# RWKV-7 bulk products of the chunks on 64x64 quarters of TensorE, in two closed bursts per head pair

## The chip, the cores and the metric

The kernel runs on one core of a Trainium2 chip. The metric is the device time of one execution in microseconds (us); for the kernel before it is the median of three runs. Five engines work side by side: TensorE (PE in the profile; its weight loads are shown apart, as PEld), VectorE (DVE), ScalarE (ACT), GpSimd (POOL) and SyncE (SP), which issues transfers. Each works through its own list of instructions in order; semaphores hold an instruction until what it reads is there. Differences under about 0.2% of the time can't be told from no change here.

## The reference

One decoder block on 512 tokens of width 2048, in float32. A projection `z = rms_norm(x) @ w_in` feeds two mixers, RWKV-7 time mixing and windowed attention, which are gated, merged, projected and followed by a gated ConvFFN. The change lies in the RWKV-7 part, with 16 heads of 64 channels:

```python
def step(state, inp):                       # state: (heads, 64, 64)
    r_t, k_t, v_t, w_t, ka_t, kb_t = inp    # ka = -kk, kb = kk * a
    sa = einsum('bhvk,bhk->bhv', state, ka_t)
    state = state * w_t[:, :, None, :] + sa[..., None] * kb_t[:, :, None, :] \
            + v_t[..., None] * k_t[:, :, None, :]
    y = einsum('bhvk,bhk->bhv', state, r_t)
    return state, y
_, y = lax.scan(step, state0, xs)           # over 512 tokens
y = group_norm(y) * gn_w + gn_b
out = (y + bonus) * g
```

## The kernel before

**Tiling.** The scan over 512 tokens is done in 8 chunks of 64 tokens (`NCH` = 8, `C` = 64), and two heads are worked on together, one in partitions 0 to 63 and one in 64 to 127: 8 head pairs. `early(p)` projects r, k and v of pair `p` and prepares decays; `late(p)` does the chunks; `final(p)` does the group norm and the output. The loop is `late(p)`, `early(p+1)`, `final(p)` and then three gate projections, and this repeats for all pairs.

**What `late` does.** For each chunk, L700 multiplies the decayed k and b vectors (`BKK`) with the decayed a and r vectors (`BAR`); L704 masks the result into four tiles: `BX` and `MD` (a head's own part) and `OA` and `MO` (which stand in the other head's rows). All of them are 128x128 per chunk; the half that doesn't belong to a head is zero. A triangular inverse is then found in `BX` by five doubling levels in float16 (L761 and L762 with weights `AI`, then with `BT`, then the transposes of L790). L737 writes the centred values `VV` with the two heads swapped, so that they meet `OA`, `MO` and `KO`.

**Bulk products.** Three sums have no dependence from chunk to chunk: `GV` = `OA` x `VV` and `KV` = `KO` x `VV` (both L724, 8 matmuls each), and the output `y` (L821 `MO` x `VV`, L822 `MD` x `UU`, L824 `BAR` x `SS`; 8 + 8 + 7 matmuls into one PSUM tile). Each is a 128x128 weight, half of it zeros, against 64 columns. `KO` shares its buffer with `OA`, so L748 and L749 clear it on POOL after the product with `OA` is done.

**The chain.** Chunk after chunk: `psG` (L802), add on DVE (L804), `psU` (L808), copy `UU` on ACT (L809), `psS` (L815), add on DVE (L816) to the next state `SS`. The products for `y` of a chunk stand in the program behind the chain's loop.

**What sets the order.** The instructions of an engine are put in order when the kernel is built, by a scheduler that simulates costs; instructions that are handed to `pin` keep their order of writing among themselves. The scheduler fills the places where the small products would wait with matmuls of the projections (`acc`, L260 to L262, 128x512), of which there are always some left: 288 per pair from the next pair's r, k, v and three gates. Weights of the projections come by DMA as `raw` and are split by ACT (`whi`, L243) and DVE (`wlo`, L244).

Of the kernel before, what the change touches and what calls it, by code (L numbers as in the profile page):

```python
# [8 lines left out]
F32 = mybir.dt.float32  # L9
# [3 lines left out]
AF = mybir.ActivationFunctionType  # L13
ALU = mybir.AluOpType
# [4 lines left out]
P = 128  # L19
# [3 lines left out]
C = 64  # L23
NCH = S // C
# [110 lines left out]
def block_kernel(ctx: ExitStack, tc: tile.TileContext, d: Dims, a: dict, out: bass.AP):  # L135
    nc = tc.nc
    act, dve, pool, pe, sync = nc.scalar, nc.vector, nc.gpsimd, nc.tensor, nc.sync
# [34 lines left out]
    K = {nm: cst[:, o - P : o - P + n] for nm, (o, n) in CONST_AT.items() if o}  # L172
# [27 lines left out]
    pin = tc.keep_in_program_order  # L200
# [80 lines left out]
    if True:  # L281
# [7 lines left out]
        with tc.tile_pool(name="x0_ps", bufs=5, space=PSUM) as ps0:  # L289
# [36 lines left out]
            r = scales(0)  # L326
# [3 lines left out]
            for k in range(NK):  # L330
                columns(0, k)
                if k == NK // 2 - 1:
                    r = scales(1)
# [55 lines left out]
        with ExitStack() as pt:  # L389
# [31 lines left out]
            for t in range(NKV):  # L421
# [16 lines left out]
                ps = small().rearrange("p (n c) -> p n c", c=P)  # L438
# [24 lines left out]
            for g in range(NHK):  # L463
# [7 lines left out]
                for n in range(NT):  # L471
# [15 lines left out]
                    st = ap_.tile([P, 4, GQ], F32, name="st", tag="st", bufs=2)  # L487
# [14 lines left out]
                    for kb in kbs:  # L502
                        ps = small().rearrange("p (h c) -> p h c", c=P)
# [6 lines left out]
                    ps = small()[:, : GQ * HD].rearrange("p (h c) -> p h c", c=HD)  # L510
                    for h in range(GQ):
                        for kb in kbs:
                            pe.matmul(ps[:, h], pT[:, kb, h], vt[:, n - 1 + kb, g * HD : (g + 1) * HD],
                                      start=kb == kbs[0], stop=kb == kbs[-1])
                    ot = ap_.tile([P, GQ, HD], F32, name="ot", tag="ot", bufs=2)
                    dve.tensor_tensor(ot, ps, rc.unsqueeze(2).to_broadcast([P, GQ, HD]), op=ALU.mult)
                    ps = small()[:, : GQ * HD].rearrange("p (j c) -> p j c", c=P)
# [7 lines left out]
        with ExitStack() as pr:  # L525
# [21 lines left out]
            def bulk():  # L547
                return blk.tile([P, S], F32, name="bulk", tag="bulk")
# [15 lines left out]
            for i in range(NG):  # L564
                acc = ztile(d.c_gd + i * P)
                t = wtile("lw")
# [12 lines left out]
            BAR = bd.tile([P, NCH, 2, 2, C], F32, name="BAR")  # L579
            pool.memset(BAR[0:C, :, :, 1], 0.0)  # L580
            pool.memset(BAR[C:P, :, :, 0], 0.0)
            MO, MD = (bd.tile([P, NCH, P], F32, name=n) for n in ("MO", "MD"))
            KD = bdtile("KD")
            SS, UU, VV, KV = (bd.tile([P, NCH, C], F32, name=n) for n in ("SS", "UU", "VV", "KV"))
            Et = bd.tile([P, NCH, C + 1], F32, name="Et")
# [9 lines left out]
            def r3(ap, c=C):  # L595
                return ap.rearrange("p (n c) -> p n c", c=c)
# [10 lines left out]
            def lora(ps, w, lo, hi):  # L607
                for i in range(lo, hi):
                    pe.matmul(ps, w[:, i], ads[:, i], start=i == lo, stop=i == hi - 1)

            def early(p):
                wl = lp.tile([P, 2 + NG, P], F32, name="wl", tag="wl", bufs=2)
# [55 lines left out]
            def late(p, st):  # L668
# [21 lines left out]
                def mb(nm, n, h=None):  # L690
                    m = K[nm] if h is None else K[nm][h[0] : h[1]]
                    return m.unsqueeze(1).to_broadcast([m.shape[0], n, m.shape[-1]])

                BKE = wk.tile([P, NCH, P], F32, name="BKE", tag="BKE")
                dve.tensor_tensor(BKE, BKK, ee.unsqueeze(2).to_broadcast([P, NCH, P]), op=ALU.mult)
                OA = wk.tile([P, NCH, P], F32, name="OA", tag="ko")
                for n0 in range(0, NCH, 2):
                    ps = bulk()
                    for j in range(2):
                        pe.matmul(ps[:, j * 4 * C : (j + 1) * 4 * C], BKK[:, n0 + j],  # L700
                                  BAR[:, n0 + j].rearrange("p a h c -> p (a h c)"), start=True, stop=True)
                    pq = ps.rearrange("p (n a c) -> p n a c", n=2, a=2)
                    for t, a, nm in ((BX, 0, "own"), (OA, 0, "other"), (MD, 1, "own"), (MO, 1, "other")):
                        dve.tensor_tensor(t[:, n0 : n0 + 2], pq[:, :, a], mb(nm, 2)[:, :, a * P : (a + 1) * P], op=ALU.mult)  # L704
                for g in range(2):
                    ns = slice(g * HN, (g + 1) * HN)
                    for h, (lo, hi) in enumerate(HV):
# [10 lines left out]
                    dve.tensor_scalar(BX[C:P, ns, C:P], tt[C:P, ns], 1.0 / SG, None, op0=ALU.mult)  # L718
                    for i in range(2):
                        dve.tensor_tensor(BT[:, i, ns], AI[:, i, ns], mb("t1bd", HN), op=ALU.mult)  # L720
                def bulk_mm(dst, l, r):
                    ps = bulk()
                    for n in range(NCH):
                        pe.matmul(r3(ps)[:, n], l(n), r(n), start=True, stop=True)  # L724
                    act.activation(dst, r3(ps), AF.Copy)

                ps = bulk()
                for t in range(NT):
                    ts = slice(t * P, (t + 1) * P)
# [2 lines left out]
                dve.reduce_sum(vm, r3(ps), axis=AX.X)  # L732
                dve.tensor_scalar(vm, vm, -1.0 / HD, None, op0=ALU.mult)
                for a, (fl, fh) in enumerate(HV):
                    for h in range(2):
                        ol, oh = HV[1 - h]
                        dve.tensor_tensor(VV[ol:oh, a::2], r3(ps)[fl:fh, h::2],  # L737
                                          vm[fl:fh, h::2].unsqueeze(2).to_broadcast([C, NT, C]), op=ALU.add)
                GV = wk.tile([P, NCH, C], F32, name="GV", tag="yt")
                bulk_mm(GV, lambda n: OA[:, n], lambda n: VV[:, n])  # L740
                for g in range(2):
                    ns = slice(g * HN, (g + 1) * HN)
                    ps = bulk().rearrange("p (n c) -> p n c", c=P)
                    for j in range(HN):
                        pe.transpose(ps[:, j], BKE[:, g * HN + j], ident)
                    if g == 0:
                        KO = wk.tile([P, NCH, P], F32, name="KO", tag="ko")
                        pool.memset(KO[0:C, :, 0:C], 0.0)  # L748
                        pool.memset(KO[C:P, :, C:P], 0.0)  # L749
                    for h, (lo, hi) in enumerate(HV):  # L750
                        ol, oh = HV[1 - h]
                        act.activation(KD[lo:hi, ns, lo:hi], ps[lo:hi, :, lo:hi], AF.Copy)
                        act.activation(KO[lo:hi, ns, ol:oh], ps[lo:hi, :, ol:oh], AF.Copy)

                bulk_mm(KV, lambda n: KO[:, n], lambda n: VV[:, n])

                def mm3(wt, both, high):
                    ps = bulk()
# [40 lines left out]
                for n in range(NCH):  # L799
                    if n:  # L800
                        ps = chn.tile([P, C], F32, name="psG", tag="chn")
                        pe.matmul(ps, BAR[:, n, 0].rearrange("p h c -> p (h c)"), SS[:, n], start=True, stop=True)  # L802
                        G = wk.tile([P, C], F32, name="G", tag="G", bufs=2)
                        dve.tensor_tensor(G, GV[:, n], ps, op=ALU.add)  # L804
                    else:
                        G = GV[:, 0]
                    ps = chn.tile([P, C], F32, name="psU", tag="chn")
                    pe.matmul(ps, BX[:, n], G, start=True, stop=True)  # L808
                    act.activation(UU[:, n], ps, AF.Copy)  # L809
                    if n == NCH - 1:  # L810
                        break
                    if n:
                        dve.scalar_tensor_tensor(KV[:, n], SS[:, n], ee[:, n : n + 1], KV[:, n], op0=ALU.mult, op1=ALU.add)
                    ps = chn.tile([P, C], F32, name="psS", tag="chn")
                    pe.matmul(ps, KD[:, n], UU[:, n], start=True, stop=True)  # L815
                    dve.tensor_tensor(SS[:, n + 1], KV[:, n], ps, op=ALU.add)  # L816

                ps = bulk()
                for n in range(NCH):
                    dst = r3(ps)[:, n]  # L820
                    pe.matmul(dst, MO[:, n], VV[:, n], start=True, stop=False)  # L821
                    pe.matmul(dst, MD[:, n], UU[:, n], start=False, stop=n == 0)  # L822
                    if n:
                        pe.matmul(dst, BAR[:, n, 1].rearrange("p h c -> p (h c)"), SS[:, n], start=False, stop=True)  # L824
                yt = wk.tile([P, NCH, C], F32, name="yt", tag="yt")
                act.activation(yt, r3(ps), AF.Copy)
                return ag, bon, yt

            def final(p, st):
                ag, bon, yt = st  # L830
                sq = wk.tile([P, NCH, C], F32, name="gn", tag="gn")
                act.activation(sq, yt, AF.Square)
                ss = wk.tile([P, NCH], F32, name="ssy", tag="ssy")
                dve.reduce_sum(ss, sq, axis=AX.X)
                rs = rsqrt_small(wk, ss, 1.0 / HD, GN_EPS)
                yd = wk.tile([P, NT, 2, C], F32, name="yd", tag="ko")
                for a, (al, ah) in enumerate(HV):
                    for h, (lo, hi) in enumerate(HV):
                        dve.tensor_tensor(yd[al:ah, :, h], yt[lo:hi, a::2],
                                          rs[lo:hi, a::2].unsqueeze(2).to_broadcast([C, NT, C]), op=ALU.mult)  # L840
                ps = bulk()
                for t in range(NT):
                    pe.transpose(ps[:, t * P : (t + 1) * P], yd[:, t].rearrange("p h c -> p (h c)"), ident)
                yc = wtile("gn")
                dve.scalar_tensor_tensor(yc, ps, col("gn_w", p), bon, op0=ALU.mult, op1=ALU.add)
                ps = bulk()
                lora(ps, ag, 1, 1 + NG)
                dve.tensor_tensor(yc, yc, ps, op=ALU.mult)
                pool.dma_start(o_rw_d[p], yc)

            st = early(0)
# [599 lines left out]
```

## Time and profile before

| | us |
|---|---|
| median of 3 runs (2877.06 to 2877.37) | 2877.19 |
| the profiled execution: its time | 2876.5 |
| the profiled execution: its span | 2874.7 |
| PE busy in the span | 2810.6 |
| DVE busy | 1957.0 |
| ACT busy | 1323.9 |
| one head pair (the third, from one L700 to the next) | 102.5 |

The span is from the first to the last instruction. A pair's length is read from the starts of its first matmul of L700, which come every 102.5 us from the second pair on. The page's "busy" counts overlapping matmuls once; their ends are modelled, so a matmul's price is better read from the distance between starts. A float32 matmul stands in the trace as two records (two passes, each with a weight load of its own), a float32r or float16 one as one. The granted TensorE clock is full in all of the span but its first part.

### The profile page before, as it was taken

Reading aid. Unit: us, or ns where it says so; the run is one execution under the profiler, and the core shown is the slowest. Engines: PE = TensorE matmul, PEld = TensorE weight load, DVE = VectorE, ACT = ScalarE, POOL = GpSimd, SP = SyncE. Lnnn points to the kernel's source line nnn. Section 1 sums busy time; section 2 is a strip of 40 time slices with the busy share of each in tenths; the row PEclk is TensorE's granted clock in tenths of the full one; section 3 lists DMA queues with packets and bytes.
Section 4 is the critical chain, followed back from the end, with each engine's and each line's share of the span. In section 5 each row is a group of like instructions: output and inputs, shape, how many; then the busy total and the mean of one; then the engine's idle time right before and its main releaser. Section 6 shows DMA issues by size and latency. Waiting matters only on the chain.

```text
span 2874.7 us, 46847 instructions
## 1 busy us (share of the span) xinstructions
PE 2810.6 (98%) x17970; PEld 2455.0 (85%) x17970; DVE 1957.0 (68%) x3388; ACT 1323.9 (46%) x2191; POOL 235.1 (8%) x319
## 2 busy tenths in 40 slices
PE   7999999999999999999999899999999999999999
PEld 6888777777777777788888899999999999888887
DVE  5566666767776675345668787777778777655655
ACT  5345344435434434322456445455555545544444
POOL 0101000000000001111000010101011010000000
PEclk9999999999999999999999999999999999999999
DMA  6855666666656657878777788888888887877775
GB/s 199 228 158 148 182 163 168 160 161 153 166 144 162 174 152 183 269 237 272 258 262 209 211 237 229 222 233 244 230 226 226 242 236 217 315 246 241 258 254 190
DMA packets 223857, 608.35 MB, mean 212 GB/s; under 512 B 24577, under 2 KB 44689, under 8 KB 222609
## 3 DMA queue, kind: packets, MB, share of 16 engines
q1 hardware_dynamic: 156096, 432.86, 46.6%
q0 software_dynamic: 36832, 134.24, 24.2%
q10 hardware_dynamic: 30704, 38.27, 3.8%
q8 instruction: 141, 2.31, 0.3%
q14 instruction: 84, 0.68, 0.1%
HBM read 554.59 MB, written 174.40 MB: 254 GB/s over the span
## 4 chain that ended last, share of the span: by engine, by line
PE 59%; DMA 3%; DVE 2%; ACT 1%; issue 1%; ACTq 0%; SPq 0%; DVEq 0%
PE X L1152 17%; PE X L1019 10%; PE Y L1019 9%; PE Y L1152 8%; PE Z L1152 4%; PE acc L262 3%; PE acc L260 3%; PE acc L261 3%; DMA raw<-in_w_z_dram 1%; DMA raw<-in_w_dn_dram 1%; DMA raw<-in_w_b_dram 0%; DMA raw<-in_w_up_dram 0%; DVE wlo L1135 0%; PE ps_t L1083 0%; DMA gate_d<-gt 0%
## 5 line engine op out<-in xcount | busy, mean ns | idle before, releaser
L260 PE MATMUL acc<-xhi,whi 128*128 128x512 f32 x1120 | 454.0, 405 | 1.9 <-ACT whi L243 1.9
L262 PE MATMUL acc<-xhi,wlo 128*128 128x512 f32 x1120 | 449.4, 401 | 3.2 <-DVE wlo L244 3.2
L261 PE MATMUL acc<-xlo,whi 128*128 128x512 f32 x1120 | 452.1, 404 | 0.0
L243 ACT ACTIVATE whi<-raw 128x512 fp32r<-128x512 f32 x352 | 219.8, 629 | 468.1 <-PE acc L261 355.0
L244 DVE TENSOR_TENSOR wlo<-raw,whi 128x512 fp32r<-128x512 f32 x352 | 240.3, 689 | 233.0 <-ACT whi L243 214.8
L1012 DVE TENSOR_TENSOR wlo<-raw,whi 128x1024 fp32r<-128x1024 f32 x210 | 257.1, 1224 | 205.3 <-ACT whi L1011 205.3
L1011 ACT ACTIVATE whi<-raw 128x1024 fp32r<-128x1024 f32 x210 | 222.6, 1060 | 289.7 <-PE X L1019 147.8
L1152 PE MATMUL X<-b,whi 128*128 128x256 f32 x1472 | 270.4, 284 | 2.3 <-DVE u L1172 0.9
L1152 PE MATMUL X<-t,whi 128*128 128x256 f32 x1408 | 259.9, 285 | 9.9 <-DVE u L1172 9.4
L1135 DVE TENSOR_TENSOR wlo<-raw,whi 128x1024 fp32r<-128x1024 f32 x176 | 215.0, 1223 | 77.8 <-ACT whi L1134 77.7
L1152 PE MATMUL Y<-t,whi 128*128 128x256 f32 x1408 | 257.1, 283 | 0.0
L262 PEld LDWEIGHTS acc<-xhi,wlo 128*128 128x128 f32 x1120 | 211.2, 189 | 45.7 <-DVE wlo L244 8.2
L260 PEld LDWEIGHTS acc<-xhi,whi 128*128 128x128 f32 x1120 | 211.7, 189 | 38.3 <-ACT whi L243 3.2
L261 PEld LDWEIGHTS acc<-xlo,whi 128*128 128x128 f32 x1120 | 211.6, 189 | 38.1 <-issue 2.2
L1134 ACT ACTIVATE whi<-a 128x1024 fp32r<-128x1024 f32 x132 | 139.4, 1056 | 218.7 <-DVE a L1128 214.6
L1152 PEld LDWEIGHTS X<-b,whi 128*128 128x128 f32 x1472 | 230.7, 193 | 3.1 <-issue 2.4
L1152 PEld LDWEIGHTS X<-t,whi 128*128 128x128 f32 x1408 | 221.7, 194 | 10.4 <-DVE u L1172 6.8
L1152 PEld LDWEIGHTS Y<-t,whi 128*128 128x128 f32 x1408 | 219.6, 192 | 0.0
L1152 PE MATMUL X<-b,wlo 128*128 128x256 f32 x736 | 209.1, 284 | 2.1 <-DVE wlo L1135 2.1
L1135 DVE TENSOR_TENSOR wlo<-a,whi 128x1024 fp32r<-128x1024 f32 x132 | 161.7, 1225 | 69.8 <-ACT whi L1134 69.2
L1152 PE MATMUL X<-t,wlo 128*128 128x256 f32 x704 | 200.4, 285 | 0.0
L1152 PE MATMUL Y<-t,wlo 128*128 128x256 f32 x704 | 199.2, 283 | 0.0
(777 smaller groups left out, 5987.4 us busy)
## 6 DMA issues: line engine op xcount, KB each, us to landing
raw<-in_w_up_dram SPq DMA_DIRECT2D x180, 512.0 KB
raw<-in_w_z_dram SPq DMA_DIRECT2D x288, 256.0 KB
s_dn<-in_w_dn_dram POOLq DMA_DIRECT2D x88, 512.0 KB, 6.8
raw<-in_w_up_dram POOLq DMA_DIRECT2D x88, 512.0 KB, 8.7
raw<-s_dn SPq DMA_DIRECT2D x88, 512.0 KB
raw<-in_w_dn_dram SPq DMA_DIRECT2D x66, 512.0 KB
a<-in_w_up_dram SPq DMA_DIRECT2D x48, 512.0 KB
s_dn<-in_w_dn_dram SPq DMA_DIRECT2D x44, 512.0 KB
```

The lines of the kernel that those rows point to most:

```text
L243: pin(act.activation(hi, raw, AF.Copy))
L244: pin(dve.tensor_tensor(lo, raw, hi.bitcast(F32), op=ALU.subtract))
L260: pe.matmul(acc, whi[:, j], xhi[:, k], start=first, stop=False)
L261: pe.matmul(acc, whi[:, j], xlo[:, k], start=False, stop=False)
L262: pe.matmul(acc, wlo[:, j], xhi[:, k], start=False, stop=last)
L1011: act.activation(whi, wr, AF.Copy)
L1012: dve.tensor_tensor(wlo, wr, whi.bitcast(F32), op=ALU.subtract)
L1019: pe.matmul(dst, l[:, q, ts], r[:, es], start=fst and j == 0, stop=lst and j == 2, skip_group_check=True)
L1134: pin(act.activation(hi, t, AF.Copy))
L1135: pin(dve.tensor_tensor(lo, t, hi.bitcast(F32), op=ALU.subtract))
L1152: pin(pe.matmul(ps, l[:, k], r[:, k], start=start and k + i == 0, stop=last and i == 2, skip_group_check=True))
```

## The change

The bulk products use 64x64 quarters of the array. A new helper `heads_mm` issues two matmuls for each one before, first for the head in partitions 64 to 127, then for that in 0 to 63; each multiplies 64 rows by 64 columns and writes 64 partitions. `OA` and `MO` become one compact tile `AM`, into which the masking (now L715 and L719) moves each part to the partitions of its own head; `KO` becomes compact too, in a buffer that needs no clearing, and `VV` is written with the heads at home. All of these matmuls are pinned, and with them the chain's `psU`. `KV` and `GV` are issued one behind the other as one burst in front of the doubling levels; the whole of `y` is taken out of the chain's neighbourhood, into `final`, as a second burst behind the chain, in reversed order of chunks, so that the last `UU` is waited for first. The chain's own products stay on the whole array.

```diff
-            MO, MD = (bd.tile([P, NCH, P], F32, name=n) for n in ("MO", "MD"))
+            MD = bd.tile([P, NCH, P], F32, name="MD")
+            AM = bd.tile([P, NCH, 2, C], F32, name="AM")
...
+            def heads_mm(dst, l, r, start, stop):
+                for h, (lo, hi) in reversed(list(enumerate(HV))):
+                    w = l[lo:hi] if l.shape[-1] == C else l[lo:hi, lo:hi]
+                    pin(pe.matmul(dst[lo:hi], w, r[lo:hi], start=start, stop=stop, skip_group_check=True))
+
+            def bulk_mm(dst, l, r):
+                ps = bulk()
+                for n in reversed(range(NCH)):
+                    heads_mm(r3(ps)[:, n], l(n), r(n), True, True)
+                act.activation(dst, r3(ps), AF.Copy)
...
-                    for t, a, nm in ((BX, 0, "own"), (OA, 0, "other"), (MD, 1, "own"), (MO, 1, "other")):
-                        dve.tensor_tensor(t[:, n0 : n0 + 2], pq[:, :, a], mb(nm, 2)[:, :, a * P : (a + 1) * P], op=ALU.mult)
+                    for t, a in ((BX, 0), (MD, 1)):
+                        dve.tensor_tensor(t[:, n0 : n0 + 2], pq[:, :, a], mb("own", 2)[:, :, a * P : (a + 1) * P], op=ALU.mult)
+                    for h, (lo, hi) in enumerate(HV):
+                        rs = slice(*HV[1 - h])
+                        mk = K["other"].rearrange("p (a c) -> p a c", a=2)[rs, :, lo:hi]
+                        dve.tensor_tensor(AM[lo:hi, n0 : n0 + 2], pq[rs, :, :, lo:hi],
+                                          mk.unsqueeze(1).to_broadcast([C, 2, 2, C]), op=ALU.mult)
...
-                    for h in range(2):
-                        ol, oh = HV[1 - h]
-                        dve.tensor_tensor(VV[ol:oh, a::2], r3(ps)[fl:fh, h::2],
+                    for h, (lo, hi) in enumerate(HV):
+                        dve.tensor_tensor(VV[lo:hi, a::2], r3(ps)[fl:fh, h::2],
...
-                GV = wk.tile([P, NCH, C], F32, name="GV", tag="yt")
-                bulk_mm(GV, lambda n: OA[:, n], lambda n: VV[:, n])
...
-                        KO = wk.tile([P, NCH, P], F32, name="KO", tag="ko")
-                        pool.memset(KO[0:C, :, 0:C], 0.0)
-                        pool.memset(KO[C:P, :, C:P], 0.0)
+                        KO = wk.tile([P, NCH, C], F32, name="KO", tag="ko")
...
+                GV = wk.tile([P, NCH, C], F32, name="GV", tag="yt")
                 bulk_mm(KV, lambda n: KO[:, n], lambda n: VV[:, n])
+                bulk_mm(GV, lambda n: AM[:, n, 0], lambda n: VV[:, n])
...
-                    pe.matmul(ps, BX[:, n], G, start=True, stop=True)
+                    pin(pe.matmul(ps, BX[:, n], G, start=True, stop=True))
...
+                return ag, bon
+
+            def final(p, st):
+                ag, bon = st
                 ps = bulk()
-                for n in range(NCH):
+                for n in reversed(range(NCH)):
                     dst = r3(ps)[:, n]
-                    pe.matmul(dst, MO[:, n], VV[:, n], start=True, stop=False)
-                    pe.matmul(dst, MD[:, n], UU[:, n], start=False, stop=n == 0)
+                    heads_mm(dst, MD[:, n], UU[:, n], True, False)
+                    heads_mm(dst, AM[:, n, 1], VV[:, n], False, n == 0)
                     if n:
-                        pe.matmul(dst, BAR[:, n, 1].rearrange("p h c -> p (h c)"), SS[:, n], start=False, stop=True)
+                        heads_mm(dst, BAR[:, n, 1].rearrange("p h c -> p (h c)"), SS[:, n], False, True)
```

Three places show how the order moves. The first is TensorE in front of the first doubling level of a pair (`BKE` feeds transposes on the whole array, `AI` the first level). Before:

```order
L724 MATMUL bulk<-VV,OA 128x64
L745 MATMUL bulk<-ident,BKE 128x128 x4
L260 MATMUL acc<-xhi,whi 128x512
L724 MATMUL bulk<-VV,OA 128x64 x7
L745 MATMUL bulk<-ident,BKE 128x128 x4
L261 MATMUL acc<-xlo,whi 128x512
L262 MATMUL acc<-xhi,wlo 128x512
L260 MATMUL acc<-xhi,whi 128x512
L261 MATMUL acc<-xlo,whi 128x512
L262 MATMUL acc<-xhi,wlo 128x512
L724 MATMUL bulk<-VV,KO 128x64 x4
L761 LDWEIGHTS AI
```

The same place in the change:

```order
L260 MATMUL acc<-xhi,whi 128x512
L261 MATMUL acc<-xlo,whi 128x512
L262 MATMUL acc<-xhi,wlo 128x512
L615 MATMUL bulk<-VV,KO 64x64 x16
L615 MATMUL bulk<-VV,AM 64x64 x16
L768 LDWEIGHTS AI
```

The 16 products were spread among transposes, projections and the first level; now 32 quarter products stand together, 29 projection matmuls behind the transposes of `BKE`, which moved ahead.

The second place is TensorE at the end of a pair's chain. Before:

```order
L808 MATMUL psU<-G,BX 128x64
L262 MATMUL acc<-xhi,wlo 128x512
L260 MATMUL acc<-xhi,whi 128x512
L261 MATMUL acc<-xlo,whi 128x512
L262 MATMUL acc<-xhi,wlo 128x512
L822 MATMUL bulk<-UU,MD 128x64
L824 MATMUL bulk<-SS,BAR 128x64
L260 MATMUL acc<-xhi,whi 128x512
```

In the change:

```order
L815 MATMUL psU<-G,BX 128x64
L260 MATMUL acc<-xhi,whi 128x512
L261 MATMUL acc<-xlo,whi 128x512
L615 MATMUL bulk<-UU,MD 64x64 x2
L615 MATMUL bulk<-VV,AM 64x64 x2
L615 MATMUL bulk<-SS,BAR 64x64 x2
L615 MATMUL bulk<-UU,MD 64x64 x2
L615 MATMUL bulk<-VV,AM 64x64 x2
```

Two products of 23 were left for this place before; now all 46 quarter products stand here. The projection matmuls between them and the transposes of `yd` (the normalised `y`) go from 34 to 27 in most pairs. Inside the doubling levels of a pair the projection matmuls that stand between the products with `AI` and those with `BT` go from 14, 15, 11, 17, 10 to 12, 10, 20, 10, 20, and those between `BT` and the transposes from 8, 10, 10, 10 to 8, 8, 8, 8.

The third place is DVE in `final`, from the sum of squares `ssy` to `yd` (`rq` are the small steps of the reciprocal root, `BKE` is the next pair's; the rows are the third pair's). Before:

```order
L834 TENSOR_REDUCE ssy<-gn 128x8
L695 TENSOR_TENSOR BKE<-BKK,ee 128x1024
L190 TENSOR_SCALAR rq_6498<-ssy 128x8
L244 TENSOR_TENSOR wlo<-raw,whi 128x512
L191 TENSOR_SCALAR rq_6500<-rq_6498 128x8
```

In the change:

```order
L707 TENSOR_TENSOR BKE<-BKK,ee 128x1024
L811 TENSOR_TENSOR G<-GV,psG 128x64
L689 SCALAR_TENSOR_TENSOR BAR<-kk,Et 64x8x64 x2
L244 TENSOR_TENSOR wlo<-raw,whi 128x512
L690 TENSOR_TENSOR BAR<-rz,Et 64x8x64 x2
L841 TENSOR_REDUCE ssy<-gn 128x8
L190 TENSOR_SCALAR rq_6606<-ssy 128x8
L191 TENSOR_SCALAR rq_6608<-rq_6606 128x8
```

`BKE` stands ahead of the chain's last `G` now, and one of the two splits of weights (`wlo`) between `ssy` and `yd` is gone from there.

More of the change, by code (lines that the diff above doesn't have):

```diff
@@ L720, in late @@
                         dve.tensor_tensor(BT[:, i, ns], AI[:, i, ns], mb("t1bd", HN), op=ALU.mult)
-                def bulk_mm(dst, l, r):
-                    ps = bulk()
-                    for n in range(NCH):
-                        pe.matmul(r3(ps)[:, n], l(n), r(n), start=True, stop=True)
-                    act.activation(dst, r3(ps), AF.Copy)
                 ps = bulk()
@@ L752, in late @@
                         act.activation(KD[lo:hi, ns, lo:hi], ps[lo:hi, :, lo:hi], AF.Copy)
-                        act.activation(KO[lo:hi, ns, ol:oh], ps[lo:hi, :, ol:oh], AF.Copy)
+                        act.activation(KO[ol:oh, ns], ps[lo:hi, :, ol:oh], AF.Copy)
+                GV = wk.tile([P, NCH, C], F32, name="GV", tag="yt")
                 bulk_mm(KV, lambda n: KO[:, n], lambda n: VV[:, n])
+                bulk_mm(GV, lambda n: AM[:, n, 0], lambda n: VV[:, n])
                 def mm3(wt, both, high):
@@ L816, in late @@
                     dve.tensor_tensor(SS[:, n + 1], KV[:, n], ps, op=ALU.add)
+                return ag, bon
+            def final(p, st):
+                ag, bon = st
                 ps = bulk()
-                for n in range(NCH):
+                for n in reversed(range(NCH)):
                     dst = r3(ps)[:, n]
-                    pe.matmul(dst, MO[:, n], VV[:, n], start=True, stop=False)
-                    pe.matmul(dst, MD[:, n], UU[:, n], start=False, stop=n == 0)
+                    heads_mm(dst, MD[:, n], UU[:, n], True, False)
+                    heads_mm(dst, AM[:, n, 1], VV[:, n], False, n == 0)
                     if n:
-                        pe.matmul(dst, BAR[:, n, 1].rearrange("p h c -> p (h c)"), SS[:, n], start=False, stop=True)
+                        heads_mm(dst, BAR[:, n, 1].rearrange("p h c -> p (h c)"), SS[:, n], False, True)
                 yt = wk.tile([P, NCH, C], F32, name="yt", tag="yt")
                 act.activation(yt, r3(ps), AF.Copy)
-                return ag, bon, yt
-            def final(p, st):
-                ag, bon, yt = st
                 sq = wk.tile([P, NCH, C], F32, name="gn", tag="gn")
```

1 line of the change is left out of this document (removed).

## The prediction

> **What bounds the kernel now.** I read the page's head and its chain first, then the busy times of one head pair (the third), then that pair's groups on TensorE.
>
> ```profile
> span 2874.7 us, 46847 instructions
> PE 2810.6 (98%) x17970; PEld 2455.0 (85%) x17970; DVE 1957.0 (68%) x3388; ACT 1323.9 (46%) x2191; POOL 235.1 (8%) x319
> ...
> PE 59%; DMA 3%; DVE 2%; ACT 1%; issue 1%; ACTq 0%; SPq 0%; DVEq 0%
> ```
> ```profile
> core 0: us, PE busy (x) PEld busy (x) DVE busy (x) ACT busy (x) POOL busy (x), PEclk, DMA share, GB/s
> 436.20:538.60 102.40, 100.29 (x662) 80.12 (x661) 72.64 (x178) 44.34 (x95) 8.11 (x11) 1.00 0.65 161
> ```
>
> TensorE works in 98% of the span and in 100.3 of the 102.4 us of a pair; DVE, next, needs 72.6 of them. So work that is taken from TensorE shortens the time, as long as projections remain to fill what was hidden behind it, and the change leaves their number as it is. In this pair the products at stake are these (a program's float32 matmul is two records):
>
> ```profile
> L821 PE MATMUL bulk<-VV,MO 128*128 128x64 f32 x16 | 3.1, 277 | 0.0
> L822 PE MATMUL bulk<-UU,MD 128*128 128x64 f32 x16 | 3.0, 272 | 0.0
> ...
> L824 PE MATMUL bulk<-SS,BAR 128*128 128x64 f32 x14 | 2.7, 275 | 0.0
> ...
> L724 PE MATMUL bulk<-VV,KO 128*128 128x64 f32 x16 | 2.2, 278 | 0.0
> L724 PE MATMUL bulk<-VV,OA 128*128 128x64 f32 x16 | 2.0, 269 | 0.0
> ```
>
> That is 16 + 16 + 14 + 16 + 16 = 78 passes a pair, 624 in all. Their means overlap; the price of one is the distance of starts, from the order of time on TensorE in the first pair:
>
> ```profile
> 352.29 1.67 PE L724 MATMUL bulk<-VV,OA 128*128 128x64 f32 x14
> 353.80 0.60 PE L745 MATMUL bulk<-ident,BKE 128*128 128x128 f32 x4
> 354.16 0.48 PE L261 MATMUL acc<-xlo,whi 128*128 128x512 f32 x1
> 354.47 0.40 PE L262 MATMUL acc<-xhi,wlo 128*128 128x512 f32 x1
> 354.70 0.40 PE L260 MATMUL acc<-xhi,whi 128*128 128x512 f32 x1
> ...
> 355.62 1.08 PE L724 MATMUL bulk<-VV,KO 128*128 128x64 f32 x8
> 356.53 0.19 PE L761 MATMUL bulk<-XIW,AI 128*128 128x64 f16 x1
> 356.56 0.18 PE L762 MATMUL bulk<-XIW,AI 128*128 128x32 f16 x1
> ...
> 356.92 0.19 PE L761 MATMUL bulk<-XIW,AI 128*128 128x64 f16 x1
> ```
>
> 14 passes take 353.80 - 352.29 = 1.51 us (0.108 each), 8 take 0.91 (0.114): 0.111 us on average.
>
> **Removed.** 624 x 0.111 = 69.3 us (67.4 to 71.1 by the two runs of passes).
>
> **Added.** Two quarter passes for each, 1248. No quarter stands in this trace, so I take a pass apart. Its load, and its stream of 64 columns:
>
> ```profile
> L377 PEld LDWEIGHTS mi<-ident,rq x10: 83/83/84, 62.4 to 218.2; 128*8 128x8 f32 x10
> ```
> ```profile
> L262 PEld LDWEIGHTS acc<-xhi,wlo 128*128 128x128 f32 x1120 | 211.2, 189 | 45.7 <-DVE wlo L244 8.2
> ```
> ```profile
> 396.76 1.02 PE L631 MATMUL bulk<-thw,wl 128*128 128x512 f32 x2
> 397.62 0.33 PE L815 MATMUL psS<-UU,KD 128*128 128x64 f32 x2
> ```
>
> A load of 8 columns shows 83 ns, one of 128 shows 189: (189 - 83) / 120 = 0.88 ns per column, 113 ns for 128 columns and 56 for 64. Two float32 passes of 512 columns start 0.86 us apart, 0.84 ns per column: 64 columns stream in 54 ns. So a whole pass (111) is bound by its load (113), and the stream runs behind it. For a quarter pass there are three prices. If the two quarters, which share neither rows nor columns of the array, load side by side, a pair of passes costs one load of 64 columns, 56 ns, or 0.028 us a pass; the float16 rows above, 15 starts in 0.39 us, show that TensorE issues a load and a matmul every 0.028 us, so issue allows just that, and no less. If the loads take turns, it is 0.056 us, what the whole array pays. Dearer is a rival below. I take 0.028, as the two heads' instructions alternate and nothing in a row ties one quarter's load to the other's: 1248 x 0.028 = 34.9 us (70 if they take turns).
>
> The Trainium skill, "TensorEngine Tiling (Array Packing)", section Key Properties, says that different tiles load and multiply in parallel; no run here shows it yet. By that sentence the added work stays 34.9.
>
> **Switches.** Two bursts a pair, each entered and left: 32 switches. Where TensorE goes from float32 to the projections, the first step is 0.31 us (354.16 to 354.47) instead of 0.23: 0.08 extra, the low bound, 2.6 us in all. The high bound is an array that empties before the first load: a matmul record (275) and a load (189), 0.46 us, 14.7 in all. I take 0.20, next to the row of the load, which then can't run ahead: 6.4 us.
>
> The same page and section say that a change of tiling mode drains TensorE, which speaks for the upper bound; with 14.7 the forecast would be some 8 us higher. No run here shows it yet.
>
> **POOL.** `KV` waited for the clearing of `KO`, which is gone; by the instructions of L724, idle time until:
>
> ```profile
>   POOL KO L749: 3.6, 8
> ```
>
> That gives back 3.6 us (0 if `KO`'s copies on ACT take its place; 29 projections, 6.7 us, stand ahead of the burst for them).
>
> **Waits in the pair.** Who TensorE waited for, in total us, times, longest:
>
> ```profile
> PE bulk L843 <- DVE yd L839: 5.1, 8, 0.6
> PE bulk L761 <- DVE XIW L207: 5.0, 16, 0.3
> PE bulk L761 <- ACT whi L243: 4.3, 16, 0.4
> ```
>
> At the pair's end the projections that cover the group norm go from 34 to 27, 7 x 0.23 = 1.6 us less. On DVE, `BKE` and one `wlo` leave this stretch:
>
> ```profile
> 419.63 1.21 DVE L695 TENSOR_TENSOR BKE<-BKK,ee 128x1024 f32<-128x1024 f32 x1
> 420.76 0.16 DVE L190 TENSOR_SCALAR rq<-ssy 128x8 f32<-128x8 f32 x1
> 420.83 0.68 DVE L244 TENSOR_TENSOR wlo<-raw,whi 128x512 fp32r<-128x512 f32 x1
> 421.44 0.16 DVE L191 TENSOR_SCALAR rq<-rq 128x8 int32<-128x8 int32 x1
> ```
>
> 1.13 + 0.61 = 1.7 us less to cover: 0, with +9.7 (six pairs) if the path doesn't get shorter. What waits behind `yd` on TensorE, were it late, are the two products of L609 and the next projections, and for those DVE. In the levels, 14, 15, 11, 17, 10 projections became 12, 10, 20, 10, 20, and 8, 10, 10, 10 became 8, 8, 8, 8. Covers of 10 and 11 now leave up to 0.3 to 0.4 us open; five short ones stay short, three shorter ones are new: I take 3 us more, with 11 (2 x 0.23 x 3 places x 8 pairs) at one end and 4 less at the other. What is late behind a level is the next level alone.
>
> **At no cost.** The masks stay 16 a pair; the moved ones read PSUM across partitions, as `VV` does, at the same price, and DVE has 30 us a pair free:
>
> ```profile
> L737 DVE TENSOR_TENSOR VV<-bulk,vm 64x256 f32<-64x256 f32 x32 | 13.5, 423 | 0.7
> ...
> L704 DVE TENSOR_TENSOR MO<-bulk,cst 128x256 f32<-128x256 f32 x32 | 13.3, 415 | 0.0
> ```
>
> The chain loses its neighbours (3 products a chunk, 0.67 us) and gets one or two projections a chunk in their place; were that cover too thin, DVE's G would be late, then `psU`. No transfer is added or moved past another. The last `UU` has two projections ahead of the burst, as each `psS` has in the chain now, and `psS` is not in that list of waits.
>
> **Sum.** - 69.3 + 34.9 + 6.4 - 3.6 + 0 + 3 = - 28.6 us. The profiled execution took 2876.5 (its span 2874.7), so 2848; the median, 2877.2, lies 0.7 higher: **2849 us**. The own range, from the nearer bounds of several terms together, is 2838 to 2864.
>
> **Rivals.** (1) *The loads take turns*, 0.056 a pass: + 35, so 2884. For it: a load's time follows its columns alone, and 2 x 64 are 128. Against: the columns lie in different rows, fed from different partitions. (2) *A quarter's load can't run beside a matmul in the same rows.* Then a product's two passes pay 54 + 56 + 54 ns, the first load hidden behind the other head: 0.164 us for each of 624 quarter products, 102 us, 67 more than forecast: 2916, slower. It decides from 0.051 us a pass on: (69.3 + 3.6 - 6.4 - 3) / 1248. Against: whole-array passes start 0.111 us apart, where load and stream in turn would need 113 + 54, so the load does run beside the matmul of the pass before. The Trainium skill, "TensorE: Matmul & The Clock Gate", section Part 3 (packing small matmuls), states this rule, that a load overlaps running matmuls only where the row group differs; the whole-array rows of this trace do not agree with it. (3) *The work goes, the waits come*: thinner cover at the pair's end (+ 9.7) and in the levels (11 instead of 3), 17.7 more: 2867. For it: every one of these places has a wait of up to 0.6 us today. Against: projections fill whatever is left, and their number is unchanged. That the change doesn't do what it says is excluded by the order: 32 and 46 quarter products stand together in every pair.
>
> **How the numbers follow.** Forecast 0.58, rival 1 0.19, rival 2 0.11, rival 3 0.12. Within 0.2% (5.8 us, what a measurement can tell from no change) lies half of rival 1: 0.10. Slower: its other half, rival 2 and a little of rival 3's tail, 0.22. Faster: 0.68. The range takes in the forecast's own, rival 3 and rival 1 with its switches at 0.3 us: 2838 to 2888; rival 2 is outside.
>
> **What will show it.** Starts of the quarter products: 32 in the first burst, two passes each, in 64 x 0.028 = 1.8 us, and the second burst of 92 passes in 2.6; twice that shows rival 1, three times rival 2. The pair's length should fall from 102.5 to 99 us. The first step into and out of a burst gives the switch. The wait of the transposes of `yd` stays near 5 us, the levels' between 5 and 20, and POOL's is gone. I am wrong if a pass costs over 0.04 us or if a pair shows new waits of over 2 us.

## The result

| | before | after |
|---|---|---|
| median of the runs, us | 2877.28 (2877.06 to 2880.60, 4 runs) | 2856.46 (2851.32 to 2857.48, 4 runs) |
| the profiled execution: time / span | 2876.5 / 2874.7 | 2857.48 / 2855.5 |
| RWKV stage, from the first matmul of `BAR`, `BKK` to the last transposes of `yd` | 806.7 | 790.6 |
| bulk products in it, distance of starts | 67.6 | 38.7 |
| projections in it, distance of starts to whatever comes next | 580.9 | 593.5 |

The ratio is 0.992, 95% interval 0.9904 to 0.9939: 21 us faster, where 28 were forecast. The last two rows add up the distances from each matmul's start to the next start on TensorE, by the kind of the first of the two. A wait of TensorE therefore counts with what ran before it, which is mostly a projection. They hold the story: the bulk products became 28.9 us cheaper, and the projections, whose number is the same, 12.6 us longer. Other kinds moved by 2.3 us or less each. The stage is 16.1 us shorter. Of the rest of the 21 us, 3.1 lie outside it in the profiled executions (1.1 ahead, 2.0 behind), where the kernels tried differ by several us from each other, and the medians differ by some 2 us more than the profiled runs do.

**The head and the pair.** From the page of the changed kernel, and from its view by stretches, whose columns are window, length and busy time (with counts) of PE, PEld, DVE, ACT and POOL, then clock and DMA:

```profile
span 2855.5 us, 48079 instructions
PE 2790.6 (98%) x18594; PEld 2421.6 (85%) x18594; DVE 1965.4 (69%) x3388; ACT 1321.3 (46%) x2191; POOL 227.2 (8%) x303
...
PE 58%; DMA 2%; DVE 1%; ACT 1%; issue 0%; ACTq 0%; POOL 0%; SPq 0%; DVEq 0%; POOLq 0%
```
```profile
435.95:536.57 100.62, 97.95 (x741) 75.93 (x739) 73.70 (x178) 43.87 (x96) 6.25 (x8) 1.00 0.65 162
```

This is the second of the eight pairs, as is the one from 436.20 that the table before and the prediction call the third. TensorE's busy time in it fell by 100.29 - 97.95 = 2.3 us, the pair by 1.8. The idle time in the pair grew from 2.1 to 2.7 us.

**The bursts.** TensorE in order of time (start, length, line, operands, tile, count), first burst of the first pair, then its second:

```profile
354.16 0.40 PE L262 MATMUL acc<-xhi,wlo 128*128 128x512 f32 x1
354.49 1.15 PE L615 MATMUL bulk<-VV,KO 64*64 64x64 f32 x32
355.47 1.10 PE L615 MATMUL bulk<-VV,AM 64*64 64x64 f32 x32
356.50 0.20 PE L768 MATMUL bulk<-XIW,AI 128*128 128x64 f16 x1
```
```profile
417.95 0.40 PE L261 MATMUL acc<-xlo,whi 128*128 128x512 f32 x1
418.28 0.33 PE L615 MATMUL bulk<-UU,MD 64*64 64x64 f32 x4
418.44 0.28 PE L615 MATMUL bulk<-VV,AM 64*64 64x64 f32 x4
...
421.11 0.50 PE L262 MATMUL acc<-xhi,wlo 128*128 128x512 f32 x1
```

32 passes start in 355.47 - 354.49 = 0.98 us, 0.031 us each; the second burst's 92 take 421.11 - 418.28 = 2.83 with the way out. The way in shows as 0.33 from the last projection's start to the burst (354.16 to 354.49, 417.95 to 418.28) where two projections start 0.23 apart.

**The waits.** Who TensorE waited for (total us, times, longest):

```profile
...
PE bulk L768 <- DVE XIW L207: 5.2, 16, 0.4
PE bulk L850 <- DVE yd L846: 3.6, 8, 0.6
PE psU L815 <- DVE G L811: 3.3, 5, 0.9
...
PE bulk L615 <- DVE VV L746: 2.1, 7, 0.3
...
PE bulk L752 <- ACT KO L758: 1.5, 7, 0.2
...
PE psG L809 <- DVE SS L823: 1.0, 1, 1.0
```

The first two rows shown were there before (5.0 and 5.1). The 4.3 us for `whi` in the levels fell to 0.6, and the wait for POOL's clearing is gone. The last four are new. The chain's `psU` and `psG`, which waited nowhere before, wait 4.3 us, and one such place, in the fourth pair, shows why. TensorE first, then VectorE:

```profile
705.90 0.40 PE L260 MATMUL acc<-xhi,whi 128*128 128x512 f32 x1
707.22 0.43 PE L815 MATMUL psU<-G,BX 128*128 128x64 f32 x2 [0.93 <-DVE G L811]
```
```profile
704.42 0.22 DVE L823 TENSOR_TENSOR SS<-KV,psS 128x64 f32<-128x64 f32 x1 [0.15 <-PE psS L822]
706.34 0.69 DVE L639 TENSOR_TENSOR kk<-kk,rsb 128x512 f32<-128x512 f32 x1 [1.70 <-DMA rsb<-rsd]
706.95 0.21 DVE L811 TENSOR_TENSOR G<-GV,psG 128x64 f32<-128x64 f32 x1
```

VectorE stands idle for 1.70 us at `kk`, a multiply of the next pair that has nothing to do with the chain: it waits for a transfer (`rsb`, the norm's factors read back as rows), and the chain's `G` is queued behind it. In the kernel before, `kk` stands at the same place of the chain, behind the third `G` and the `SS` that follows it, and starts without a wait, here in the second pair:

```profile
506.66 0.22 DVE L816 TENSOR_TENSOR SS<-KV,psS 128x64 f32<-128x64 f32 x1
506.79 0.68 DVE L627 TENSOR_TENSOR kk<-kk,rsb 128x512 f32<-128x512 f32 x1
```

Idle time ahead of `kk`, from the view of the tile `rsb`, before and after:

```profile
  DVE kk L627: 0.5, 1
```
```profile
  DVE kk L639: 10.7, 8
```

### The profile page after: what moved, and what is told of

Same layout as the page of the kernel before. It is cut to its first block, busy times and chain, and to the rows that moved or that the text cites. A ratio compares the mean times of both kernels' runs of the same rounds, so it can differ in the third digit from the quotient of the medians.

```text
span 2855.5 us, 48079 instructions
## 1 busy us (share of the span) xinstructions
PE 2790.6 (98%) x18594; PEld 2421.6 (85%) x18594; DVE 1965.4 (69%) x3388; ACT 1321.3 (46%) x2191; POOL 227.2 (8%) x303
## 4 chain that ended last, share of the span: by engine, by line
PE 58%; DMA 2%; DVE 1%; ACT 1%; issue 0%; ACTq 0%; POOL 0%; SPq 0%; DVEq 0%; POOLq 0%
PE X L1159 18%; PE X L1026 11%; PE Y L1026 9%; PE Y L1159 8%; PE Z L1159 4%; PE acc L262 2%; PE acc L261 2%; PE acc L260 2%; DMA raw<-in_w_z_dram 1%; DVE wlo L1142 0%; DMA raw<-in_w_up_dram 0%; DMA h_o<-gin 0%; ACT whi L1141 0%; PE ps_t L1090 0%; DMA s_dn<-s_dn 0%
```

## The experiments

Each kernel was timed against the kernel before on the same chip. The first four ran beside 2876.07 us for it (2871.59 to 2882.15, 17 runs), the other four beside 2875.73 (2870.52 to 2880.51, 23 runs).

| kernel | us | ratio to before, 95% |
|---|---|---|
| whole_bursts | 2878.51 | 0.9999 to 1.0023 |
| same_quarter | 2884.13 | 1.0015 to 1.0041 |
| scattered | 2867.39 | 0.9950 to 0.9976 |
| kk_after4 | 2847.54 | 0.9879 to 0.9909 |
| after_again | 2856.36 | 0.9915 to 0.9952 |
| before_kk4 | 2877.01 | 0.9996 to 1.0015 |
| chain_quarters | 2883.60 | 1.0018 to 1.0042 |
| kk4_burst_late | 2874.02 | 0.9988 to 1.0008 |

**Bursts and order without quarters** (whole_bursts).

```diff
-                for h, (lo, hi) in reversed(list(enumerate(HV))):
-                    w = l[lo:hi] if l.shape[-1] == C else l[lo:hi, lo:hi]
-                    pin(pe.matmul(dst[lo:hi], w, r[lo:hi], start=start, stop=stop, skip_group_check=True))
+                pin(pe.matmul(dst, l, r, start=start, stop=stop, skip_group_check=True))
```

`OA`, `MO` and `VV` are as in the kernel before; `KO` is built in the buffer of `BKE`, cleared by POOL.

> The change with its bursts and its order of TensorE, but each bulk product as one matmul on the whole array again (block tiles with zeros, as in the kernel before; KO built in the buffer of BKE, so that nothing waits for a late clearing). Theory 'the quarters are the gain': the passes go back from 0.031 to 0.111 us, 624 x 0.111 - 38.7 = + 30 us on the changed kernel, 2882 to 2890, no better than the kernel before. Rival 'the order is the gain' (closed bursts, y out of the chain, no clearing in front of KV): within 5 us of the changed kernel's 2856.

Measured 2878.51 us: no change against before, and 3.5 us under the theory's range, far from the rival's 2856. The profiled execution took 2884.32, near the slowest of the ten. TensorE in order of time, first burst:

```profile
356.69 1.97 PE L613 MATMUL bulk<-VV,BKE 128*128 128x64 f32 x16
358.50 1.95 PE L613 MATMUL bulk<-VV,OA 128*128 128x64 f32 x16
```

16 passes in 358.50 - 356.69 = 1.81 us, 0.113 each. So the gain is the quarters', and the grouping with its new order wins nothing by itself. The order already brings part of the new waits: the projections' sum is 587.2 us here, 6.3 of the 12.6 more, and VectorE stands idle at `kk` for 9.4 us. (Entry into a burst is 0.23 at its shortest here, so the 0.33 above belongs to the quarters.)

**One head after the other** (same_quarter): in each of the three sums all products of one head, then all of the other, so that neighbours share a quarter. The first burst so has four runs of 16 passes: `KO` for one head, `KO` for the other, and the same with `AM`.

```diff
+                for h in (1, 0):
+                    for n in reversed(range(NCH)):
+                        heads_mm(r3(ps)[:, n], l(n), r(n), True, True, h)
...
+                for h, n in ((h, n) for h in (1, 0) for n in reversed(range(NCH))):
```

> The same quarter products in the same bursts, but all of one head first and then all of the other, so that neighbours load into the same quarter. Theory 'two quarters load side by side': a load now waits for the one before it, 0.056 us a pass in place of 0.031, 1248 x 0.025 = + 31 us, 2883 to 2891. Rival 'a load of 64 columns is simply cheaper than its columns say' (or issue alone sets 0.031): no change, 2851 to 2860. Rival 'a load waits for the matmul in the same rows': 0.11 us a pass, + 99 us, 2955.

Measured 2884.13 us, ratio 1.003, in the theory's range. TensorE in the first burst, from the end of the products with `KO` on:

```profile
357.14 0.22 PE L615 MATMUL bulk<-VV,KO 64*64 64x64 f32 x1
357.20 1.67 PE L615 MATMUL bulk<-VV,AM 64*64 64x64 f32 x29
358.80 0.20 PE L769 MATMUL bulk<-XIW,AI 128*128 128x64 f16 x1
```

29 passes in 1.60 us: 0.055 each, against 0.031 when the heads alternate. Within one run the starts lie 0.058 apart; where one run follows another in the other quarter they overlap. In the first burst of the change, too, the starts of one quarter lie 0.058 apart (0.008 and 0.050 in turn). So the two quarters work side by side, and neither slows the other. Which limit sets the 0.058 is not shown: the prediction's estimates for a load (56 ns) and for a stream (54 ns) are too close to tell. The second rival's price in the prediction, 0.164 for a product of two passes in one quarter with the other head's work beside it, falls: two passes in one quarter took 2 x 0.058 = 0.116.

**Quarters without bursts** (scattered): the sum for `y` stands beside the chain again, in order of chunks, with no pins.

```diff
-                    pin(pe.matmul(dst[lo:hi], w, r[lo:hi], start=start, stop=stop, skip_group_check=True))
+                    pe.matmul(dst[lo:hi], w, r[lo:hi], start=start, stop=stop, skip_group_check=True)
...
-                    pin(pe.matmul(ps, BX[:, n], G, start=True, stop=True))
+                    pe.matmul(ps, BX[:, n], G, start=True, stop=True)
```

> The quarters without the closed second burst: y stands beside the chain again, in ascending order of chunks and unpinned, so that a pair has some 9 groups of quarter products (8 of them between matmuls on the whole array) in place of 2; the first burst comes out as in the change. Theory 'a switch costs about 0.1 us in and little out': 7 more groups x 8 pairs x 0.1 to 0.2 = + 6 to + 11 us, 2860 to 2870, less what thinner waits at the pair's end give back. Rival 'a switch empties the array, 0.46 us each way': 112 x 0.46 = + 52 us, 2908. Rival 'nothing': 2851 to 2858.

Measured 2867.39 us, in the theory's range, though a group cost more than its 0.1 to 0.2 us and a wait that it did not count went. There are 56 more groups of quarters in the stage (seven a pair), and the distances of starts grow by 8.2 us in the bulk products, 7.3 in `psS` and 2.4 in `psG`, which now stand next to them: 17.9 us, 0.32 for a group's way in and out, with whatever wait falls there. The projections' sum falls by 10.7 us (582.8): `psU` and `psG` are out of the list of waits, and `kk`, which the scheduler has put two `G` later on VectorE, waits 0.4 us in all. So the closed bursts are worth 11 us against the changed kernel, which has the wait at `kk`, and 20 us (2867.39 to 2847.54) against the next run, which has it no more; the second is near the 17.9.

**The wait at `kk` taken away** (kk_after4): the multiply is issued on VectorE behind `G` of the chain's fifth chunk, when `rsb` is there.

```diff
-                dve.tensor_tensor(kk, kk, rb, op=ALU.mult)
+                with tc.issue_after(held_["g"]) if held_ else ExitStack():
+                    dve.tensor_tensor(kk, kk, rb, op=ALU.mult)
...
-                        dve.tensor_tensor(G, GV[:, n], ps, op=ALU.add)
+                        g_ = dve.tensor_tensor(G, GV[:, n], ps, op=ALU.add)
+                        if n == 4:
+                            held_["g"] = g_.ins
```

> The change, with one multiply on DVE (kk by its reciprocal norm, which comes back through DRAM) issued behind the fifth G of the chain instead of before it. Theory 'the chain waits for that transfer because DVE is in order': the waits of psU and psG (4.3 us in the changed kernel's profile) go, 2850 to 2854, and the pairs get equally long. Rival 'the wait moves': the next G or the next pair's BKK is late instead, and the time stays at 2855 to 2858.

Measured 2847.54 us (2846.57 to 2849.12, 4 runs), 9 us below the changed kernel, 2 us under the theory's range and the fastest here. Who TensorE waited for:

```profile
...
PE bulk L771 <- DVE XIW L207: 5.1, 16, 0.4
PE bulk L855 <- DVE yd L851: 4.7, 8, 0.6
...
PE bulk L615 <- DVE VV L749: 2.1, 7, 0.3
...
PE bulk L755 <- ACT KO L761: 1.6, 8, 0.2
```

`psU` and `psG` are out of the list, and from the second pair on all take 99.7 to 100.0 us, where the changed kernel's take 99.5 to 100.7. The stage is 784.7 us, 5.9 less than the changed kernel's (4.7 less than in after_again, the same kernel once more, with 789.4), and the projections' sum is 5.7 less. That is about what the wait at `kk` was worth. Another 5 us lie behind the stage, nearly all in the projections up to the ConvFFN (229.8 us instead of 234.5); two gaps of TensorE between projections are gone there (2.0 and 0.8 us between starts), and the rest of that I did not break down. That stretch lies between 230 and 238 us in the kernels tried, so it is not shown that the edit wins it. The edit holds back one instruction; the scheduler then orders others behind it differently as well, on VectorE and on TensorE.

**The same in the kernel before** (before_kk4; the changed kernel ran again beside it, as after_again).

> The changed kernel as it is, on the chip of the next three, so that they can be compared with it. Expected: 0.992 of the kernel before, about 2855 us.

> The kernel before, with the multiply of kk by the rows read back (rsb) issued on VectorE behind the addition that makes G of the chain's fifth chunk, as in kk_after4. Theory: the stall of VectorE on the rsb transfer is something the change brought, since the kernel before shows only 1.8 us of it in 2 places, so there is little to win here: 2872 to 2877 us. Rival: the place of kk is simply a better order for the chain in either kernel, and is worth the 9 us here too that it was worth in the changed one: about 2867 us.

Measured 2877.01 us, a ratio of 1.0005, at the upper end of the theory's range. The edit wins nothing where the stall isn't: this is a wait that the change brought, and not a better order in general. (Of the 1.8 us of waits for `rsb` in the kernel before that the expectation names, 0.5 is at `kk`.) after_again came to 2856.36.

**The chain on quarters too** (chain_quarters): `psG`, `psU` and `psS` go through `heads_mm`.

```diff
-                    pin(pe.matmul(ps, BX[:, n], G, start=True, stop=True))
+                    heads_mm(ps, BX[:, n], G, True, True)
```

> The changed kernel with the chain's products psG, psU and psS on two quarters each as well. They are 22 products, 44 passes, per pair. Price of a pass from the bursts: 0.031 us a quarter, so 0.062 instead of 0.111 for a pass, 44 x 0.049 = 2.2 us less per pair. Theory: each of them stands alone between whole-array projections, and the run with scattered quarters gave about 0.32 us for going into a group and out: 22 x 0.32 = 7.0 us more per pair, net +4.9 x 8 = 39 us, of which the projections' slack may give some back: 2878 to 2895 us, slower than the changed kernel. Rival: most of those 0.32 us were the waits that the scattered products caused, and a group alone costs the 0.15 us of a burst's entry and exit: 3.3 us per pair, net +1.1 x 8 = 9 us, 2860 to 2868. Second rival: leaving and entering costs nothing, -17 us, 2839.

Measured 2883.60 us, 27 more than the changed kernel. TensorE around one `psU`, there and in the changed kernel:

```profile
401.14 0.40 PE L261 MATMUL acc<-xlo,whi 128*128 128x512 f32 x1
401.47 0.33 PE L615 MATMUL psU<-G,BX 64*64 64x64 f32 x4
401.73 0.50 PE L262 MATMUL acc<-xhi,wlo 128*128 128x512 f32 x1
402.06 0.39 PE L260 MATMUL acc<-xhi,whi 128*128 128x512 f32 x1
```
```profile
400.97 0.40 PE L262 MATMUL acc<-xhi,wlo 128*128 128x512 f32 x1
401.20 0.33 PE L815 MATMUL psU<-G,BX 128*128 128x64 f32 x2
401.34 0.48 PE L260 MATMUL acc<-xhi,whi 128*128 128x512 f32 x1
401.66 0.40 PE L261 MATMUL acc<-xlo,whi 128*128 128x512 f32 x1
```

From the projection ahead to the second one behind it is 0.92 us with quarters and 0.69 whole: the way in costs 0.10 (0.33 for 0.23), the product with the way out 0.12 (0.26 for 0.14), the projection behind 0.01. Over all 176 such products the medians are 0.093, 0.09 and 0.02. A whole product of two passes takes 0.055 to 0.16 us between its two starts and is out 0.084 later, so there is little a quarter could save on it. This run shows no wait at `psU`: VectorE stands at `kk` for 1.3 us in all, not 10.7. In six of the seven pairs with a chain ahead of `kk`, the scheduler has put `kk` one `G` later, where kk_after4 has it.

So the fairer neighbour is kk_after4, and against it the quarters cost 36 us, which is what the medians give: 176 x (0.093 + 0.09 + 0.02) = 35.7. The theory's time came true by luck: its 0.32 a group was too much, and so were the 2.2 us a pair that it took off for cheaper passes.

**A later first burst** (kk4_burst_late): kk_after4 with the two `bulk_mm` calls for `KV` and `GV` written behind the first doubling level.

> kk_after4 with the first burst (VV by KO, VV by AM) written behind the first doubling level instead of ahead of it. Theory: TensorE's waits at the burst for VV (2.1 us) and at the transposes of BKE for KO's copies (1.6 us) go, 3.7 us at most, and the levels start earlier: 2843 to 2848 us. Rival: KV and GV, that the burst makes, are then late for the chain, or the levels wait more because the burst no longer covers them: 2850 to 2860 us.

Measured 2874.02 us; the gain is lost. Who TensorE waited for, and one such place in the second pair, on TensorE and on VectorE:

```profile
...
PE acc L262 <- DVE wlo L244: 11.6, 9, 1.6
...
PE bulk L769 <- DVE XIW L207: 7.2, 15, 2.7
...
PE psG L813 <- DVE SS L829: 4.1, 5, 1.2
```
```profile
457.85 0.50 PE L262 MATMUL acc<-xhi,wlo 128*128 128x512 f32 x1 [1.56 <-DVE wlo L244]
```
```profile
455.01 1.72 DVE L749 TENSOR_TENSOR VV<-bulk,vm 64x256 f32<-64x256 f32 x4
456.77 0.43 DVE L790 TENSOR_TENSOR half__4740<-half__4740,cst 128x256 f32<-128x256 f32 x1
457.11 0.69 DVE L244 TENSOR_TENSOR wlo<-raw,whi 128x512 fp32r<-128x512 f32 x1
```

Neither theory foresaw this place: with the burst moved, `VV` runs on VectorE ahead of a projection's `wlo`, and the projection waits for that, by 1.55 us in each of seven pairs. The time lies in the rival's direction and well above its 2860. The 2 us at `VV` were not to be had this way.

## Why the prediction was right, and which step was off

The time, 2856, lies in the predicted range, and in the forecast's own of 2838 to 2864; the direction was right. The size was further off than the time shows: all 28.6 us of the sum lie in the RWKV stage, and the stage gave 16.1. The rest of the 21 us belongs to no step of the sum, so that it came this near is partly luck. Of the signs given at the end of the prediction, those of the products held: a pass costs 0.031 us, and the bursts take 2.0 and 2.83 us where 1.8 and 2.6 were forecast. The pairs take 99.5 to 100.7 us from the second on, where 99 was forecast. In those pairs the projections' sum grew by 0.9 to 2.0 us. In the first pair it grew by 4.0, over the 2 us that were to show an error; before_kk4, without the change, has 2.5 more there too. Step by step:

**Removed work: right.** 69.3 us forecast. Measured 67.6 for the bulk products, and 2.3 for the `psS`, which stood next to them before: 69.9. The 2.3 come from the order, as whole_bursts has them too (9.8 us for the `psS`, as in the change).

**Added work: right.** 0.028 us a pass forecast, 0.031 measured: 38.7 us instead of 34.9. Many starts come 0.007 us behind the one before (the other quarter's) and the next then 0.052 later; others are spaced more evenly, 0.023 and 0.036. What decides is that both quarters work at once, as same_quarter shows. The Trainium skill, "TensorEngine Tiling (Array Packing)", Key Properties, says the same of tiles, and the trace agrees with it (0.031 alternating, 0.055 in one quarter). The Trainium skill's rule in "TensorE: Matmul & The Clock Gate", Part 3, that a load overlaps a running matmul only where the row group differs, doesn't fit same_quarter either: load (56 ns) and stream (54), as the prediction estimates them, would be 0.110 a pass one after the other, and 0.058 was measured within a quarter.

**Switches: over twice too much.** 6.4 us forecast for 32, 0.20 each. The medians of the lone groups in chain_quarters, without the product itself, are 0.093 on the way in, 0.064 from the last start to the projection (0.148 instead of 0.084) and 0.02 behind it: 0.18 for in and out, 2.9 us for 16 groups. That is the lower bound (0.08 a switch), not the row of the load. Part of it stands in the 38.7 above already (the way out). Work and switches together were forecast as 41.3, and came to 38.7 + 16 x 0.093 + some 0.2 = 40.4.

**POOL, the pair's end and the levels: sizes off.** The row of 3.6 us for POOL's clearing was misread: it is idle time of the weight loads, not of the matmuls, and it isn't in TensorE's list of waits. One of the eight places, on PEld:

```profile
355.58 0.97 PEld L724 LDWEIGHTS bulk<-VV,KO 128*128 128x128 f32 x8 [0.46 <-POOL KO L749]
```

From the projection ahead to the first product with `KO` TensorE took 0.43 to 0.45 us, 0.2 more than between two projections: 1.7 us in eight pairs at most, and not 3.6. In the change that step is 0.33 in the first pair and 0.68 to 0.70 in the other seven, since it now waits for `VV`:

```profile
455.39 0.39 PE L260 MATMUL acc<-xhi,whi 128*128 128x512 f32 x1
456.08 0.53 PE L615 MATMUL bulk<-VV,KO 64*64 64x64 f32 x11 [0.30 <-DVE VV L746]
```

So this place got dearer. The wait for `yd` is 3.6 instead of 5.1, and the levels' waits fell from 9.3 to under 6, where I took 3 us more.

**Waits: the step that failed.** Work and switches, 40.4 - 69.9 = - 29.5 us, would have given the forecast. The other three terms of the sum (- 3.6 + 0 + 3) are - 0.6 together; the stage shows + 13.4 in their place, nearly all in the projections. The projections' sum is 12.6 us longer, and 1.5 of that is the way into the bursts; some 11 us are waits. By what comes behind the projection, against before: `psU` 4.6 us, the transposes of `BKE` 3.5, the products of `BAR` and `BKK` 2.7, other projections 2.6, the bursts 1.7 with the ways in; less in the levels (0.9) and at `yd` (1.5). About 1.3 of the 2.7 is a single wait for `bon` in the first pair, which differs from run to run (1.1 us in after_again, 2.7 in before_kk4, 0.4 before). Two sentences of the part "At no cost" were wrong:

- *The chain's neighbours.* I wrote that the cover might be too thin, and that `G` would be late then, and ruled it out by the absence of `psS` in the list of waits. What is late isn't the chain's own path: `G` waits on VectorE behind `kk`, and `kk` for another pair's transfer. The chain now starts sooner in a pair: its first `psU` comes 58.1 us behind the first product of `BAR` and `BKK`, where it came 60.4 before (pairs 2 to 7). VectorE is free for `kk` at 68.5 us and not at 70.6, while the transfer of `rsb` is issued no sooner, at 66.4 to 67.2 in five of these six pairs (66.5 to 67.5 in all six before); in the sixth, at 63.4, the wait at `kk` is only 0.2 us. From the first `psU` to `kk` the chain takes 10.2 us before and 10.4 now. So it isn't the missing products of `y` between the chain's steps that bring it there early (more projections stand there in their place), but what became shorter ahead of it; in whole_bursts, by the order alone, the first `psU` already comes at 58.8. kk_after4 and before_kk4 together show that the wait costs time: holding `kk` back gives 5 to 6 us of the stage (9 in all) in the changed kernel and nothing in the kernel before. I said that no transfer is moved past another, which is so, but I didn't ask who stands behind a transfer's reader.
- *The masks at the same price.* The length of one is the same as before, but the starts lie further apart. VectorE in order of time in the first pair:

```profile
334.02 0.41 DVE L715 TENSOR_TENSOR BX<-bulk,cst 128x256 f32<-128x256 f32 x1
334.36 0.68 DVE L676 TENSOR_TENSOR bon<-vz,bulk 128x512 f32<-128x512 f32 x1
334.95 0.42 DVE L715 TENSOR_TENSOR MD<-bulk,cst 128x256 f32<-128x256 f32 x1
335.38 0.86 DVE L719 TENSOR_TENSOR AM<-bulk,cst 64x256 f32<-64x256 f32 x2
336.27 0.42 DVE L715 TENSOR_TENSOR BX<-bulk,cst 128x256 f32<-128x256 f32 x1
```

  `bon` starts 0.34 us behind `BX`, the first `AM` 0.43 behind `MD`, and the two `AM` with what follows take 0.89. Over the stage, a mask over 128 partitions is followed by the next such one after 0.33 to 0.34 us (`BX` by `MD` here, all four before), and an instruction over 64 partitions by one over the other 64 after 0.42 to 0.45 (`AM`, `VV`, and `tt`, which moves nothing across partitions). `OA` and `MO` were of the first kind; `AM` is of the second. What makes the difference is not shown: the step from `MO` to `tt`, from 128 partitions to 64, took 0.33 before, that from `MD` to `AM` takes 0.43. I had read the price off the lengths, where the two look alike. With 0.10 to 0.12 us at three steps of each of four groups that is about 1.3 us a pair on VectorE, just ahead of the transposes and the first burst. Whether the waits for `VV` (2.1 us) and for `KO`'s copies (1.5) come from that was not tried; whole_bursts, with the old masks, waits for `VV` as well (3.0), so they are not the whole of it.

The third rival, that waits come in place of work, was right in kind and got a chance of 0.12. It looked for them at the pair's end and in the levels, and there they fell. The first rival is refuted by 0.031 us a pass, the second by same_quarter.

**What stays open:** how the 3.5 us at `BKE` and the rest of the 2.7 at `BAR`, `BKK` divide among masks, copies and order (whole_bursts has none of the 3.5, with the old masks in the new order, so the order alone doesn't make them), and what makes the 5 us that kk_after4 has less behind the stage.

## What to carry to other kernels

When half of a weight is zeros and the two blocks share neither rows nor columns, two quarters that alternate took 0.062 us here for what a whole pass took 0.111 (bound by its load, by the prediction's estimate); keep them in closed groups, and leave single products of two passes on the whole array, where the way in and out (0.18 us here) is more than they can save. When a change lets a chain start sooner, look at every instruction that stands ahead of the chain's steps on the in-order engines, above all those that wait for a transfer: their data may now come later than the chain does. Here holding back that one instruction was enough to end the wait.

## What the runs showed of the hardware that was not expected

In a group of alternating quarters, starts of two quarters lie as little as 6 to 8 ns apart. In same_quarter, where the products with `KO` end in one quarter, records of the first ones with `AM`, in the other, lie among the last of them (starts at 356.98, 357.08 and 357.14 among 357.03, 357.09 and 357.14): the second quarter did not wait for the first to be done. And on VectorE, two masks or copies on different halves of the partitions start 0.42 to 0.45 us apart where two masks over all partitions, of the same length (0.42), start 0.33 apart: a length alone is not a price.
